# Layer 1's output projection with five chunks in space of their own, activation tables asked for ahead of use, and a reordered layer norm with filler transposes

## The chip, the core and the metric

The kernel runs on one NeuronCore of a Trainium2 chip. [...] The metric is the device time of one execution in microseconds; lower is better.

## The reference, cut to what matters

A decoder of two layers over 256 tokens of 1024 features, in fp32. Each layer is: a token mixer together with a memory cross-attention, one output projection, a residual and a layer norm, then a PEER channel mixer (a product-key expert layer), a residual and a layer norm.

```python
for i in range(2):
    z  = x @ w_in[i]                                   # streams of the mixer and the 4 attention queries
    hm = mlstm(z) if i == 0 else rglru(z)              # 768 of 1024 features
    ha = cross_attention(xq, mem, w_kv[i])             # the other 256
    x  = layer_norm(ALPHA * x + concat(hm, ha) @ w_out[i])   # "ln1"
    x  = layer_norm(ALPHA * x + peer_ffn(x))                 # "ln2"; starts with q = x @ w_q
```

Layer 1's mixer is a gated linear recurrence. Per channel, with r and i sigmoids of two block-diagonal projections of the convolved stream:

```python
log_a = -8 * r * softplus(-lam); a = exp(log_a)
u = sqrt(-expm1(2 * log_a)) * (i * xr)
h[t] = a[t] * h[t-1] + u[t];  y = h * gelu(gate)
```

## The kernel before, in words

Every large product is done on split operands: a weight `w` is cast to `wH` (a rounded fp32 form that PE runs at full rate) and `wL = w - wH`, the moving operand likewise, and `mm3` (L168 to L172) issues three matmuls, HH, LH and HL. All weights come by one list of items in the order of use. `load` (L119) issues their DMAs on SP into a ring of five raw buffers, `pump` (L78) casts (ACT, or DVE with `cast_dve`) and subtracts (DVE, POOL for the first `pool_cols` columns), and `next` (L137) hands one split item to the products and keeps the splitting three items ahead. Split items live in a ring of three, except those with a destination of their own: the third to fifth chunk of each `w_out` go to `self.extra` (`EXTRA = 3`). There is no scheduler: every queue's order is the order of the Python calls. Small generators placed beside a projection (`beside`, `tick`) get one step per weight item, after its splitting.

**The output projection** is `proj_n` (L188). It runs over the eight 128-row chunks of `w_out` in the order given by `ORDER`. With `tail`, the last chunks are held back: first all products of token half 0 (two banks of 512 columns) over those chunks, then those of token half 1 (banks of 512, 256 and 256 columns), and between these the layer norm's generator `norm` (L260) is stepped, so that half 0 is normalized beside half 1's products. Layer 0 holds back six chunks, layer 1 four. For half 1, the chunks in the ring come ahead of those in space of their own.

**The norm** (`early` form, L263 to L411): residual add and statistics per bank (`add`, `half`, L275 to L283), square root on ACT (L288), reciprocal (L291). Half 0's first 256 columns are scaled by ACT and POOL (`scale_beside`, L308 to L312), the next 256 by DVE (`center` L296, `spread` L301) and transposed (`turn`, L322, copies L225 and L226) beside half 1's products. After half 1's statistics, its first 256 columns are scaled and transposed; that is what the first query projection of the PEER layer (`proj_t`, 24 matmuls of 256 columns per weight item) waits for. Half 0's columns 512 to 1023 are scaled after that and transposed by later steps, beside the projection.

**Layer 1's mixer** (`rglru_layer`, L709): six block projections on PE (L229), sigmoids on ACT (L827), then for three pairs of channel groups b = 0, 1, 2: `decay(b)` (POOL multiplies i by the stream, L793; ACT takes exp and tanh, L794 and L795; DVE forms the argument of the square root, L796 and L797), `root(b)` (ACT, L801), `scan(b)` (DVE, L804 and L806) and `mixed(b)` (DVE gate product L810, cast and subtract into `mixH` and `mixL`). ACT holds one table of functions at a time; sigmoid, exp with tanh, and the square root each need their own load. The attention's transposes, copies (L490) and products stand between the parts of b = 0. `scan(2)` and `mixed(2)` are called inside the output projection, ahead of its fifth chunk, and so behind the splitting of the last three chunks on DVE and ACT.

Of the kernel before, what the change touches and what calls it, by code (L numbers as in the profile page):

```python
# [7 lines left out]
F32 = mybir.dt.float32  # L8
# [5 lines left out]
ALU = mybir.AluOpType  # L14
# [4 lines left out]
P = 128  # L19
# [15 lines left out]
MIX_COLS = 0  # L35
GAP, GAP2 = 56, 104
ORDER = [(6, 7, 0, 1, 2, 3, 4, 5), (0, 1, 6, 7, 2, 3, 4, 5)]
CAND = [(0, 1, 16, 0), (1, 1, 8, 16), (2, 1, 5, 24), (3, 1, 4, 29), (4, 1, 3, 33), (5, 3, 2, 36), (8, 8, 1, 42)]
# [7 lines left out]
class Trunk:  # L46
# [91 lines left out]
    def next(self, ahead=HL_BUFS):  # L138
        while callable(self.items[self.n_got][2]) or self.items[self.n_got][3] is not None:
            self.pump(self.n_got + 1)  # L140
            self.split.pop(self.n_got, None)
            self.n_got += 1
        i = self.n_got
        self.pump(i + ahead)
        self.n_got += 1
        self.tick()
        return self.split.pop(i)
# [14 lines left out]
    pool_cols = MIX_COLS  # L162
    put_off = None
    chained = False
# [19 lines left out]

    def proj_n(self, splits, stat, order=range(DT), tail=0, hook=(-1, None)):
# [12 lines left out]
        last = (DT - 1, DT - 1 - HL_BUFS if tail else DT - 1)  # L198
        for n, dt in enumerate(order):
            if n == hook[0]:  # L200
                hook[1]()
            late.append((n, dt, self.next(min(HL_BUFS + min(n, EXTRA), DT - n) if tail else HL_BUFS)))
            if n + 1 > DT - tail and n + 1 < DT:
                continue
            if tail and n + 1 == DT:
                break
            for tt in range(2):
                for k in range(len(parts[tt])):
                    products(tt, k, late)
            late = []  # L210
        if not tail:
            return banks
        ln = self.norm(banks, False, True)
        own, ring = late[:tail - HL_BUFS], late[tail - HL_BUFS:]
# [42 lines left out]
    def norm(self, y, last, early, fill=False):  # L257
# [71 lines left out]
        if last:  # L329
# [24 lines left out]
        nc.vector.tensor_scalar(nm, mv[:, 0, 0:1], rs[:, 0:1], -1.0, op0=ALU.mult, op1=ALU.mult)  # L354
# [5 lines left out]
        if fill:  # L360
            owed = []
            self.pool_cols, self.put_off = 512, owed.append
            self.pump(self.n_got + 3)
            self.put_off = None
        else:
# [29 lines left out]
        root(1)  # L395
        spread(1, 0, 1)
        turn(1, 0, 1)
        scale(1, 1, 1)
        scale(0, 2, 2), scale(1, 2, 2)
        self.release("g", "b")  # L400

        def rest():
            yield
            turn(1, 1, 1)
            yield
            turn(0, 2, 2)
            yield
            turn(1, 2, 2)
        self.beside(rest())

# [101 lines left out]
    def mlstm_layer(self):  # L512
        nc, tc, A = self.nc, self.tc, self.A
        with ExitStack() as ctx:
# [185 lines left out]
            def turn():  # L700
                for k in range(3):
# [6 lines left out]
                    self.split_to(self.flat2(self.mixH, k), self.flat2(self.mixL, k), p)  # L708
            self.proj_n((512, 512), (self.mixH, self.mixL), ORDER[0], HL_BUFS + EXTRA, (2, turn))  # L709


    def rglru_layer(self):
        nc, tc, A = self.nc, self.tc, self.A
        with ExitStack() as ctx:
# [49 lines left out]
            def values():  # L764
                for c in (2, 3):
# [12 lines left out]
            self.extra = [(w2.tile([P, D], F32R, name=f"eH{i}"), w2.tile([P, D], F32R, name=f"eL{i}"))  # L778
                          for i in range(EXTRA)]
            rr = w2.tile([P, 2, 6, T], F32, name="rr")  # L780
            aa = w2.tile([P, 6, T], F32, name="aa")
            th = w2.tile([P, 6, T], F32, name="th")
            for b in range(3):
                nc.scalar.activation(gt[:, 2 * b:2 * b + 2, :].rearrange("p a b -> p (a b)"), gb[b], AF.Gelu)
            dve = nc.vector.tensor_copy
            self.cast_dve = True
            self.pump(self.n_got + 2 + EXTRA)
            self.cast_dve = False
            fl = lambda t, b: t[:, 2 * b:2 * b + 2, :].rearrange("p a b -> p (a b)")

            def decay(b):
                for i in (2 * b, 2 * b + 1):
                    nc.gpsimd.tensor_mul(rr[:, 1, i, :], xc[:, i, :], rr[:, 1, i, :])  # L793
                    nc.scalar.activation(aa[:, i, :], rr[:, 0, i, :], AF.Exp, scale=c8[:, i:i + 1])  # L794
                    nc.scalar.activation(th[:, i, :], rr[:, 0, i, :], AF.Tanh, scale=n8[:, i:i + 1])  # L795
                nc.vector.tensor_mul(fl(rr[:, 0], b), fl(aa, b), fl(aa, b))  # L796
                nc.vector.scalar_tensor_tensor(fl(th, b), fl(rr[:, 0], b), 1.0, fl(th, b),  # L797
# [393 lines left out]
    def plan(self):  # L1191
# [24 lines left out]
        def tail(layer):  # L1216
            for i, dt in enumerate(ORDER[layer]):
                self.add(A["w_out"][layer, dt], D, i - 2 if 0 <= i - 2 < EXTRA else None)
            norm("ln1", layer)
# [119 lines left out]
```

## Time and profile before

| | us |
|---|---|
| median of three runs (1837.09 to 1838.29) | 1837.71 |
| the profiled execution, its own time | 1837.36 |
| span of its trace | 1835.5 |
| PE busy in the span | 1805.2 |
| DVE, ACT, POOL busy | 1301.6, 942.6, 430.2 |

The span runs from the first instruction to the last; the profiled execution's own time lies 1.9 us above it, and 0.35 us under the median. Times in rows of the timeline are microseconds from the span's start: start, length, engine, line, operation, output and inputs; a bracket gives the idle time of that engine just before and whose instruction ended it. Rows of PE in the timeline are pipelined, so that two of them overlap and the distance of their starts is what one costs. In rows of the windows, the columns are the stretch, its length, busy time (and count) of PE, the granted PE clock (1.00 is full), the share of DMA time and GB/s. A row of the waits is: who waited for whom, total us, times, longest us.

### The profile page before, as it was taken

The page shows a single profiled execution, that of the slowest core. Times are in us where ns is not written, and L with a number is a line of the kernel's source. Part 1 is how long each engine was busy: PE and PEld are TensorE (multiplying, and loading weights), DVE is VectorE, ACT ScalarE, POOL GpSimd, SP SyncE. Part 2 cuts the span into 40 slices and gives each one's busy share as a digit, 9 for nine tenths or more (in the row PEclk, how much of TensorE's full clock was granted, in tenths as well). Part 3 has the DMA queues.
Part 4 walks back from the last instruction along what each step waited for, and adds up shares of the span by engine and source line. Part 5 has one row for each costly group of instructions (what it writes and reads, how often), then busy time and mean ns, then how long its engine had stood idle before and what let it go on. Part 6 is the DMA issues. An engine that isn't in the chain of part 4 may idle for free.

```text
span 1835.5 us, 33243 instructions
## 1 busy us (share of the span) xinstructions
PE 1805.2 (98%) x12756; PEld 1666.0 (91%) x12756; DVE 1301.6 (71%) x2659; ACT 942.6 (51%) x1613; POOL 430.2 (23%) x324
## 2 busy tenths in 40 slices
PE   8999999999999999999999899999999999999998
PEld 8999999999999888888898799999999988888886
DVE  6673679599998555666678648785999965555556
ACT  6554555455544555555557355554555454555443
POOL 2015762433331000100001368335333300000000
PEclk9999999999999999999999899999999999999999
DMA  7655566655555666667644355666555566666664
GB/s 238 205 159 187 173 195 189 195 171 162 162 162 170 195 192 193 193 218 228 206 167 150 119 174 182 195 195 186 161 162 161 162 183 195 194 192 193 192 195 136
DMA packets 95551, 334.19 MB, mean 182 GB/s; under 512 B 10652, under 2 KB 13728, under 8 KB 95136
## 3 DMA queue, kind: packets, MB, share of 16 engines
q1 hardware_dynamic: 93752, 328.93, 58.7%
q10 hardware_dynamic: 1640, 3.15, 0.5%
q8 instruction: 99, 1.62, 0.4%
q14 instruction: 60, 0.49, 0.1%
HBM read 330.98 MB, written 1.05 MB: 181 GB/s over the span
## 4 chain that ended last, share of the span: by engine, by line
PE 72%; issue 17%; POOL 7%; DVE 2%; ACT 1%; DMA 1%; SPq 0%; POOLq 0%; DVEq 0%; ACTq 0%
PE bank L172 23%; PE bank L170 23%; PE bank L171 23%; POOL wL L108 7%; PE bank L229 2%; DMA raw<-in_w0kg_dram 0%; ACT wH L98 0%; PE bank L322 0%; POOL wL L111 0%; DVE wL L113 0%; DVE x L275 0%; SPq L127 0%; DVE x L296 0%; DMA cp<-in_rg_par_dram 0%; DVE x L301 0%
## 5 line engine op out<-in xcount | busy, mean ns | idle before, releaser
L98 ACT CAST wH<-raw 128x1024 fp32r<-128x1024 f32 (+2 forms) x607 | 628.6, 1037 | 772.3 <-PE bank L172 321.0
L113 DVE TENSOR_TENSOR wL<-raw,wH 128x1024 fp32r<-128x1024 f32 (+3 forms) x413 | 464.8, 1128 | 446.4 <-ACT wH L98 433.6
L170 PE MATMUL bank<-xHL,wH 128*128 128x256 f32 x2536 | 717.3, 283 | 7.1 <-ACT wH L98 6.2
L172 PE MATMUL bank<-xHL,wL 128*128 128x256 f32 x2536 | 703.9, 278 | 0.6 <-DVE wL L113 0.5
L171 PE MATMUL bank<-xHL,wH 128*128 128x256 f32 x2536 | 704.2, 278 | 0.0
L170 PEld LDWEIGHTS bank<-xHL,wH 128*128 128x128 f32 x2536 | 478.9, 189 | 7.9 <-ACT wH L98 6.2
L172 PEld LDWEIGHTS bank<-xHL,wL 128*128 128x128 f32 x2536 | 478.7, 189 | 1.4 <-DVE wL L113 1.0
L171 PEld LDWEIGHTS bank<-xHL,wH 128*128 128x128 f32 x2536 | 479.4, 189 | 0.4 <-DVE xHL L226 0.3
L171 PE MATMUL bank<-wL,cH 128*128 128x512 f32 x1015 | 394.3, 388 | 0.0
L170 PE MATMUL bank<-wH,cH 128*128 128x512 f32 x1015 | 394.3, 388 | 0.0
L172 PE MATMUL bank<-wH,cL 128*128 128x512 f32 x1015 | 394.3, 388 | 0.0
L111 POOL TENSOR_TENSOR wL<-raw,wH 128x1024 fp32r<-128x1024 f32 (+1 forms) x121 | 257.3, 2129 | 212.3 <-ACT wH L98 211.4
L171 PEld LDWEIGHTS bank<-wL,cH 128*128 128x128 f32 x1015 | 190.5, 188 | 39.6
L170 PEld LDWEIGHTS bank<-wH,cH 128*128 128x128 f32 x1015 | 190.5, 188 | 39.2
L172 PEld LDWEIGHTS bank<-wH,cL 128*128 128x128 f32 x1015 | 190.5, 188 | 39.1
L108 POOL TENSOR_TENSOR wL<-raw,wH 128x386 fp32r<-128x386 f32 x126 | 129.5, 1027 | 280.1 <-DVE wL L106 280.1
L311 POOL TENSOR_TENSOR x<-x,raw 128x256 f32<-128x256 f32 x6 | 4.8, 803 | 559.9 <-ACT x L308 559.9
L966 DVE TENSOR_TENSOR oh<-iota,i12T 128x1024 f16<-128x1024 f16 x128 | 130.4, 1018 | 0.0
L106 DVE TENSOR_TENSOR wL<-raw,wH 128x640 fp32r<-128x640 f32 x126 | 104.0, 825 | 7.6
L969 DVE TENSOR_TENSOR oh<-oh,gT 128x1024 f16<-128x1024 f16 x128 | 90.0, 703 | 4.4
L1099 PE MATMUL bank<-oh 128*128 128x128 f16 x1024 | 80.9, 220 | 1.1 <-DVE oh L969 1.1
L1099 PEld LDWEIGHTS <-oh 128*128 128x128 f16 x1024 | 58.8, 97 | 6.0 <-DVE oh L969 1.5
(276 smaller groups left out, 1534.3 us busy)
## 6 DMA issues: line engine op xcount, KB each, us to landing
raw<-in_u_dram SPq DMA_DIRECT2D x256, 512.0 KB, 3.6
raw<-in_v_dram SPq DMA_DIRECT2D x256, 512.0 KB, 4.3
raw<-in_w_q_dram SPq DMA_DIRECT2D x32, 512.0 KB, 3.9
raw<-in_w_out_dram SPq DMA_DIRECT2D x16, 512.0 KB, 4.1
raw<-in_w0qx_dram SPq DMA_DIRECT2D x8, 512.0 KB, 5.0
raw<-in_wkv_dram SPq DMA_DIRECT2D x8, 512.0 KB, 4.6
raw<-in_w0v_dram SPq DMA_DIRECT2D x8, 384.0 KB, 6.2
raw<-in_w0o_dram SPq DMA_DIRECT2D x8, 384.0 KB, 3.1
```

The source lines that it names most:

```text
L98: (nc.vector.tensor_copy if self.cast_dve else nc.scalar.copy)(h[:, c], r[:, c])
L106: nc.vector.tensor_sub(l[:, k:], r[:, k:], h[:, k:].bitcast(F32))
L108: nc.gpsimd.tensor_sub(l[:, :k], r[:, :k], h[:, :k].bitcast(F32))
L111: nc.gpsimd.tensor_sub(l[:, :k], r[:, :k], h[:, :k].bitcast(F32))
L113: rest = lambda l=l, r=r, h=h, k=k: nc.vector.tensor_sub(l[:, k:], r[:, k:], h[:, k:].bitcast(F32))
L170: mm(out, sH, mH, start=start, stop=False, skip_group_check=True)
L171: mm(out, sH, mL, start=False, stop=False, skip_group_check=True)
L172: mm(out, sL, mH, start=False, stop=stop, skip_group_check=True)
L229: self.nc.tensor.matmul(out, lhsT, rhs, start=start, stop=stop, skip_group_check=True)
L966: nc.vector.tensor_tensor(flat(oh[:, 1:3]), self.iota2.unsqueeze(1).to_broadcast([P, 4, P, 2]), pairs(self.i12T[:, j]), op=ALU.is_equal)
L969: nc.vector.tensor_tensor(flat(oh[:, 0:2]), two.rearrange("p z (q e t) -> p z q e t", q=2, t=2), pairs(self.gT[:, j]), op=ALU.mult)
L1099: nc.tensor.matmul(wp[:, qs], oh[:, 2, q // 2, :, q % 2], oh[:, z, q // 2, :, q % 2], start=z == 0, stop=z == 1, skip_group_check=True)
```

## The change

Five edits.

1. `EXTRAS = (3, 5)`: layer 1's `w_out` has five chunks in space of their own instead of three, its first seven chunks are split before the products start (two more by DVE, ahead of `decay(0)`), and layer 1 holds back five chunks instead of four. In half 1 one ring chunk is followed by four own chunks (before: three and one).
2. Layer 1's mixer is reordered. One-element activations ask for the sigmoid table right after the gelus and for the square root's table right after the exponentials; `decay` is cut into ACT's and POOL's part and DVE's part `grown`; `scan(0)` stands ahead of the attention's copies; `scan(2)` and `mixed(2)` come before the output projection instead of inside it; the casts of `mixed(1)` and `mixed(2)` move from ACT to DVE.
3. The early norm, both layers: all of half 0 is scaled (DVE columns 256 to 1023) and transposed beside half 1's products. Half 1's first two 128-column pieces are scaled, transposed and copied one by one, with 22 filler transposes of the identity on PE ahead of them and 5 behind. One of the two weight splits issued there gives POOL 512 instead of 1024 columns, with DVE's part called later.
4. The remaining transposes are stepped by `ahead`, before the splitting of the next item instead of after it.
5. At the start, the first two pieces of `x` transposed are loaded into raw buffers instead of into `qT`'s space.

```diff
+FILL = (22, 5)
+EXTRAS = (EXTRA, 5)
@@ next
         i = self.n_got
+        if self.ahead:
+            next(self.ahead, None)
         self.pump(i + ahead)
@@ proj_n
-        last = (DT - 1, DT - 1 - HL_BUFS if tail else DT - 1)
+        n_ring = DT - 2 - extra
+        last = (DT - 1, DT - 1 - n_ring if tail else DT - 1)
-        own, ring = late[:tail - HL_BUFS], late[tail - HL_BUFS:]
+        own, ring = late[:-n_ring], late[-n_ring:]
+    def idle(self, n):
+        b = self.bank()
+        for _ in range(n):
+            self.nc.tensor.transpose(b[:, :P], self.ident, self.ident)
@@ norm
-        if early:
-            root(0)
-            scale(0, 1, 1)
-        else:
+        if fill:
             yield
             part = add(1, 0)
-            root(0)
+        root(0)
         nc.vector.tensor_scalar(nm, mv[:, 0, 0:1], rs[:, 0:1], -1.0, op0=ALU.mult, op1=ALU.mult)
         scale_beside(0, 1 if early else 2)
         if early:
+            scale(0, 1, 1), scale(0, 2, 2)
             yield
             part = add(1, 0)
         half(*part)
-            self.pool_cols = D
-            self.pump(self.n_got + 4)
+        owed = []
+        if early:
+            self.pool_cols = D
+            self.pump(self.n_got + 3)
+        self.pool_cols, self.put_off = 512, owed.append
+        self.pump(self.n_got + 3 + early)
+        self.put_off = None
         if early:
-            turn(0, 0, 2)
+            turn(0, 0, 2), turn(0, 2, 2)
...
         center(1, 0, 1)
         root(1)
-        spread(1, 0, 1)
-        turn(1, 0, 1)
+        ps = [self.bank() for _ in range(2)]
+        for dt in range(2):
+            ds = slice(dt * P, (dt + 1) * P)
+            nc.vector.scalar_tensor_tensor(x[:, 1, ds], x[:, 1, ds], rs[:, 1:2], b[:, ds], op0=ALU.mult, op1=ALU.add)
+        self.idle(FILL[0])
+        for dt in range(2):
+            nc.tensor.transpose(ps[dt][:, :P], x[:, 1, dt * P:(dt + 1) * P], self.ident)
+            nc.scalar.copy(self.xH[:, dt, P:], ps[dt][:, :P])
+        for dt in range(2):
+            nc.vector.tensor_sub(self.xL[:, dt, P:], ps[dt][:, :P], self.xH[:, dt, P:].bitcast(F32))
+        self.idle(FILL[1])
+        owed.pop()()
         scale(1, 1, 1)
-        scale(0, 2, 2), scale(1, 2, 2)
+        scale(1, 2, 2)
@@ rglru_layer
+            nc.scalar.activation(junk, self.eps, AF.Sigmoid)
-            self.cast_dve = True
-            self.pump(self.n_got + 2 + EXTRA)
-            self.cast_dve = False
+
+            def early(n):
+                self.cast_dve = True
+                self.pump(self.n_got + n)
+                self.cast_dve = False
+            early(5)
@@ 
-            decay(0)
-            root(0)
+            early(7)
+            decay(0), nc.scalar.activation(junk, self.eps, AF.Sqrt)
+            grown(0), root(0), scan(0)
             self.xattn_turn(w2, dve)
             for co in range(3, 6):
                 gate(co, rest[co - 3])
-            scan(0)
             first, last = self.xattn_out(0), self.xattn_out(1)
             mixed(0, dve)
             self.split_to(*first, dve)
+            decay(1), decay(2), nc.scalar.activation(junk, self.eps, AF.Sqrt)
+            for b in (1, 2):
+                grown(b), root(b)
             self.split_to(*last, dve)
-            for b in (1, 2):
-                decay(b)
-            for b in (1, 2):
-                root(b)
-            scan(1)
-            mixed(1)
-            self.proj_n((512, 512), (self.mixH, self.mixL), ORDER[1], HL_BUFS + 1,
-                        (4, lambda: (scan(2), mixed(2))))
+            scan(1), mixed(1, dve)
+            scan(2), mixed(2, dve)
+            self.proj_n((512, 512), (self.mixH, self.mixL), ORDER[1], 5, EXTRAS[1])
@@ plan
-            to.stage = lambda dt=dt: self.qT[:, dt, :]
+            if dt > 1:
+                to.stage = lambda dt=dt: self.qT[:, dt, :]
```

More of the change, by code (lines that the diff above doesn't have):

```diff
@@ L162 @@
     pool_cols = MIX_COLS
-    put_off = None
+    put_off = ahead = None
     chained = False
@@ L183, in proj_t, with proj_n @@
         return banks
-    def proj_n(self, splits, stat, order=range(DT), tail=0, hook=(-1, None)):
+    def proj_n(self, splits, stat, order=range(DT), tail=0, extra=EXTRA, hook=(-1, None)):
         sH, sL = stat
@@ L201, in proj_n @@
                 hook[1]()
-            late.append((n, dt, self.next(min(HL_BUFS + min(n, EXTRA), DT - n) if tail else HL_BUFS)))
+            late.append((n, dt, self.next(min(HL_BUFS + min(n, extra), DT - n) if tail else HL_BUFS)))
             if n + 1 > DT - tail and n + 1 < DT:
@@ L359, in norm @@
         half(*part)
-        if fill:
-            owed = []
-            self.pool_cols, self.put_off = 512, owed.append
+        owed = []
+        if early:
+            self.pool_cols = D
             self.pump(self.n_got + 3)
-            self.put_off = None
-        else:
-            self.pool_cols = D
-            self.pump(self.n_got + 4)
+        self.pool_cols, self.put_off = 512, owed.append
+        self.pump(self.n_got + 3 + early)
+        self.put_off = None
         self.pool_cols = MIX_COLS
         if early:
-            turn(0, 0, 2)
+            turn(0, 0, 2), turn(0, 2, 2)
         yield
@@ L405, in rest @@
             yield
-            turn(0, 2, 2)
             yield
             turn(1, 2, 2)
-        self.beside(rest())
+            yield
+            self.ahead = None
+        self.ahead = rest()
     def mem_k(self, kb, c, h, l):
@@ L708, in turn @@
                     self.split_to(self.flat2(self.mixH, k), self.flat2(self.mixL, k), p)
-            self.proj_n((512, 512), (self.mixH, self.mixL), ORDER[0], HL_BUFS + EXTRA, (2, turn))
+            self.proj_n((512, 512), (self.mixH, self.mixL), ORDER[0], HL_BUFS + EXTRA, EXTRA, (2, turn))
     def rglru_layer(self):
@@ L778, in rglru_layer @@
             self.extra = [(w2.tile([P, D], F32R, name=f"eH{i}"), w2.tile([P, D], F32R, name=f"eL{i}"))
-                          for i in range(EXTRA)]
+                          for i in range(EXTRAS[1])]
             rr = w2.tile([P, 2, 6, T], F32, name="rr")
@@ L795, in decay, with grown @@
                     nc.scalar.activation(th[:, i, :], rr[:, 0, i, :], AF.Tanh, scale=n8[:, i:i + 1])
+            def grown(b):
                 nc.vector.tensor_mul(fl(rr[:, 0], b), fl(aa, b), fl(aa, b))
@@ L1217, in tail @@
             for i, dt in enumerate(ORDER[layer]):
-                self.add(A["w_out"][layer, dt], D, i - 2 if 0 <= i - 2 < EXTRA else None)
+                self.add(A["w_out"][layer, dt], D, i - 2 if 0 <= i - 2 < EXTRAS[layer] else None)
             norm("ln1", layer)
```

## The prediction

> **What bounds the kernel now.** I read the page first, then PE's waits, then the timeline around each of them, then the granted clock in windows. The page (PE's row of its first part, and a DMA row):
>
> ```profile
> PE 1805.2 (98%) x12756; PEld 1666.0 (91%) x12756; DVE 1301.6 (71%) x2659; ACT 942.6 (51%) x1613; POOL 430.2 (23%) x324
> ...
> raw<-in_w_out_dram SPq DMA_DIRECT2D x16, 512.0 KB, 4.1
> ```
>
> PE is idle for 2% of the span, some 30 us, so an edit away from PE's gaps is worth nothing. PE's waits over the whole span name nearly all of those gaps:
>
> ```profile
> PE bank L322 <- DVE x L301: 7.3, 3, 4.1
> PE bank L170 <- ACT wH L98: 6.2, 1, 6.2
> PE bank L170 <- ACT mixH L225: 3.3, 1, 3.3
> PE bank L170 <- DVE mixH L225: 2.2, 1, 2.2
> ```
>
> L322 is a transpose of the early norm (one wait in layer 0, two in layer 1), 6.2 is the kernel's start, and both `mixH` rows are layer 1's mixer. The change edits exactly these places. Idle time has a second price, shown by the granted clock (fourth column; the third is PE's busy time):
>
> ```profile
> 136.03:139.44 3.41, 1.46 (x13) 1.00 0.49 151
> ...
> 142.85:146.27 3.42, 3.42 (x18) 0.50 0.02 6
> ...
> 1002.99:1006.40 3.41, 1.99 (x8) 1.00 0.00 0
> ...
> 1016.65:1020.06 3.41, 1.39 (x7) 1.00 0.88 276
> ...
> 1023.47:1026.89 3.42, 3.42 (x9) 0.50 0.02 5
> ...
> 1040.55:1043.96 3.41, 3.41 (x17) 0.50 0.20 67
> ```
>
> The clock halves at the end of a 3.41 us stretch in which PE was busy 1.39 or 1.46 us, and not after one with 1.99 us; it comes back at the end of a fully busy stretch. So three times (layer 0's norm, layer 1's mixer, layer 1's norm) some 4 to 6 us of matmuls run at 0.50.
>
> [...]
>
> **Layer 1's mixer.** Timeline rows, times in us:
>
> ```profile
> 978.86 8.45 SPq L127 DMA_DIRECT2D raw<-in_w_out_dram  x5
> ...
> 986.87 0.69 DVE L98 CAST eH<-raw 128x1024 fp32r<-128x1024 f32 x1
> ...
> 988.74 0.69 DVE L98 CAST eH<-raw 128x1024 fp32r<-128x1024 f32 x1
> ...
> 994.86 0.69 DVE L796 TENSOR_TENSOR rr<-aa 128x512 f32<-128x512 f32 x1 [3.78 <-ACT th L795]
> ...
> 996.36 1.28 ACT L801 ACT_TABLE_LOAD   x1 [1.53 <-DVE th L797]
> ...
> 997.65 0.72 ACT L801 ACTIVATE th<-th,tiny 128x512 f32<-128x512 f32 x1
> ...
> 997.45 2.48 DVE L490 COPY pT<-bank 128x512 f32<-128x512 f32 x4 [1.18 <-PE bank L487]
> ...
> 1003.43 0.83 DVE L225 CAST mixH<-gt 128x512 fp32r<-128x512 f32 x1
> ...
> 1004.41 0.47 PE L170 MATMUL bank<-wH,mixH 128*128 128x512 f32 x1 [2.23 <-DVE mixH L225]
> ...
> 1007.47 0.40 PE L170 MATMUL bank<-wH,mixH 128*128 128x512 f32 x1
> ...
> 1010.25 0.40 PE L170 MATMUL bank<-eH,mixH 128*128 128x512 f32 x1
> ...
> 1014.46 3.50 DVE L113 TENSOR_TENSOR wL<-raw,wH 128x1024 fp32r<-128x1024 f32 x3 [0.26 <-ACT wH L98]
> ...
> 1018.59 1.27 DVE L806 TENSOR_TENSOR_SCAN aa<-aa,th 128x256 f32<-128x256 f32 x2
> ...
> 1021.29 0.79 PE L170 MATMUL bank<-wH,mixH 128*128 128x512 f32 x1 [3.25 <-ACT mixH L225]
> ```
>
> *Two more chunks split early.* One cast with its subtraction costs DVE 1.87 (start to start of the casts), two 3.74. They fall into the 3.78 that DVE idles before 994.86: cost 0. Without that cover everything behind on DVE would slip. SP issued the last `w_out` loads by 987.3, and one lands in 4.1, so the data are there.
>
> *Table loads.* The square root of b = 0 waited 1.28 for its table (996.36 to 997.64) after DVE had finished. Asked for right after the tanh, the load runs beside `grown(0)`: 1.3 saved on that path, and again before `root(1)`. The early sigmoid saves nothing, for the block products behind it set the time. POOL's multiplies move only with ACT. [...]
>
> *DVE's chain, rewritten,* with 0.69 for every 512-column operation: `grown(0)` ends at 996.25, its root at 997.0, `scan(0)` (0.69 + 1.27) at 998.95, the four copies at 1001.45, `mixed(0)`'s product and cast at 1002.95. PE starts there instead of at 1004.41. Then: its subtraction 0.69, first attention split 0.76 (half of 0.83 + 0.69), `grown(1)` and `grown(2)` 2.76, second split 0.76, `scan(1)` 1.96, `mixed(1)` 2.21, `scan(2)` 1.96, product and cast of `mixed(2)` 1.52: 1015.55. The 0.83 was taken while POOL ran; the 1024-column cast takes 0.69, so 512 columns may cost 0.35. I take the middle for the last two: `mixed(2)` at 1015.1, bounds 1014.6 to 1016. Before, it came at 1021.29, held by the three splits (3.50) and the ACT cast, which are gone from its path.
>
> *PE.* A chunk costs 2.78 (1007.47 to 1010.25), each half of its columns for each token half 0.69. Three chunks from 1002.95, 0.2 for `mixL`, and three shares of 0.69 end at 1013.6; then a new wait of 1.5 for `mixed(2)` in place of 3.25. Behind it stand 0.69, four shares of bank 1 (2.78) and the ring chunk (1.39), plus 0.2 for `mixL`: half 0 ends at 1020.2.
>
> **The norms.** Timeline, layer 1, the last three rows layer 0:
>
> ```profile
> 996.82 1.91 PE L487 MATMUL bank<-ident,pr 128*128 128x128 f32 x16
> ...
> 1027.63 0.69 DVE L275 SCALAR_TENSOR_TENSOR x<-x,bank 128x512 f32<-128x512 f32 x1 [1.96 <-PE bank L172]
> ...
> 1030.90 0.60 ACT L308 ACTIVATE x<-x,nm,rs 128x256 f32<-128x256 f32 x1 [1.29 <-DVE nm L354]
> ...
> 1032.39 0.73 POOL L312 TENSOR_TENSOR x<-x,raw 128x256 f32<-128x256 f32 x1
> ...
> 1034.49 0.69 DVE L226 TENSOR_TENSOR xHL<-bank,xHL 128x512 fp32r<-128x512 f32 x1 [0.50 <-ACT xHL L225]
> ...
> 1038.69 0.69 PE L322 MATMUL bank<-ident,x 128*128 128x128 f32 x2 [4.14 <-DVE x L301]
> ...
> 1039.84 0.58 PE L170 MATMUL bank<-xHL,wH 128*128 128x256 f32 x1 [0.46 <-ACT xHL L225]
> ...
> 1041.07 1.77 DVE L296 SCALAR_TENSOR_TENSOR x<-x,mv,raw 128x512 f32<-128x512 f32 x1
> ...
> 1042.88 0.75 DVE L301 SCALAR_TENSOR_TENSOR x<-x,rs,raw 128x512 f32<-128x512 f32 x1
> ...
> 137.72 0.40 DVE L275 SCALAR_TENSOR_TENSOR x<-x,bank 128x256 f32<-128x256 f32 x1
> ...
> 140.15 0.66 PE L322 MATMUL bank<-ident,x 128*128 128x128 f32 x2 [2.65 <-DVE x L301]
> ...
> 141.27 0.58 PE L170 MATMUL bank<-xHL,wH 128*128 128x256 f32 x1 [0.46 <-ACT xHL L225]
> ```
>
> *Layer 1.* The add of bank 1 waits for bank 0's add and statistics: 1020.9 instead of 1027.63, 6.7 earlier. ACT's scale came 3.27 after it; two 256-column operations (about 0.95) move behind it, so 1023.25, and POOL's products, 2.2 later, at 1025.5. DVE then does that pair (1024.2) and the new 512-column pair: 0.75 + 0.75 quiet, 1.77 + 0.75 as beside POOL; I take 1026.4. PE reaches the transposes at 1020.2 + 1.39 + 2.78 = 1024.4, so a second new wait of 1.6 to 2 (before: 0.7). A transpose costs 0.11 (1.91 for 16, less the last one's tail), eight 0.9; 24 matmuls follow and end at 1029.6. DVE: add and statistics 1.4, two subtractions 1.38, the next quarter 0.8: the last quarter's add at 1030.0. From that add to the first query matmul layer 0 took 3.55 (137.72 to 141.27); with 128-column pieces and transposes at full clock I take 3.2: restart at 1033.2 against 1039.84, **6.6 saved**.
>
> *Fillers.* 22 of 0.11 are 2.4: 1029.6 to 1032.0, while the first piece comes at about 1032.2, so they delay nothing; the five behind run beside the copy and the subtraction. If DVE were sooner, each would cost 0.11. They keep PE busy through the gap, so the clock should stay: the stretch at 0.50 ran from 1039.84 to 1043.96, half of it is **2.05 saved**. The moved transposes of half 0 leave the busy stream for waiting time, **0.4 saved**.
>
> *Layer 0.* No mixer gain, and one subtraction of 0.69 more ahead of the last add: restart at 138.4 + 3.2 = 141.6, **0.3 lost**; the clock (141.27 to 146.27 at half) **2.5**, the transposes **0.4 saved**. Its six held chunks cover the new 512-column pair.
>
> *Splits.* POOL's load drops by half a split and DVE takes it later, 0.69; with the clock full, PE also reaches the third weight item 2 us sooner, and DVE's queue is then just in time: **0.3 lost**. `ahead` puts the transposes' copies before the casts on ACT, which costs nothing there, as PE is 2.8 behind.
>
> **The start.** Timeline:
>
> ```profile
> 1.29 0.29 DVE L249 CAST iota<-fi 128x256 f16<-128x256 int32 x1
> ...
> 1.61 0.39 SPq L127 DMA_DIRECT2D qT<-in_xT_dram  x1
> ```
>
> `qT` lies on space that the constants' setup used, and the first DMA goes out right after DVE's last use of it (1.58). A raw buffer has no such past. Bounds: 1.6 if SP is free from the span's start, nothing if something else holds it as long. I take the middle, **0.8**, as all of PE's first wait (6.2) hangs on that DMA. The fourth and fifth weight loads now wait for the first two splits, and land later by at most half a microsecond, 1 us before PE needs them.
>
> **Sum.** 6.6 + 2.05 + 0.4 (layer 1), 2.6 (layer 0), 0.8, less 0.3: 12.1. The profiled execution took 1837.36, 0.35 under the median: 1825.3, on the median's footing 1825.5.
>
> **Rivals.**
> *A: the two new waits of layer 1 cost the clock.* 1.5 and 1.6 us in a 3.41 stretch leave 1.8 to 1.9 busy, between the 1.46 that lost it and the 1.99 that kept it. One loss is 1.7 to 2.5, both 4: 1829.5.
> *B: the fillers don't hold the clock.* They read one constant tile, and no row shows transposes alone. Then they run at half rate, some 2.9 longer in each layer, and 2.5 and 2.05 are not saved: 10.4 dearer, 1836. [...]
> *C: the mixer gains less.* If DVE's chain meets POOL throughout, `mixed(2)` comes 3 to 4 later: 1829.
> *D: slower.* DVE's queue stands behind the two early casts: if their loads came late by S, decay, scans, products, norm all slip by S. It decides from S = 12 for no gain, 16 for 0.2% slower: 1842. Against it: 4.1 to landing, and five raw buffers whose turn comes by 987.
>
> **How the numbers follow.** Forecast 0.70 (alone 1821.5 to 1829), A 0.12, B 0.06, C 0.05, D 0.07. The bound of what can be told from no change is 0.2%, 3.7 us. Faster: forecast, A, C and half of B, 0.90; same: half of B, 0.03; slower: D, 0.07. The range 1821 to 1833 holds forecast, A and C with the unknown cast, contention and start; B, D and the tails are left out.
>
> **What would show it.** Right: DVE busy without a gap from 991 to 995; no table load between DVE's `grown` and the root; `mixH`'s last cast about 6 us earlier, on DVE; PE's waits 1 to 2 us in the mixer and at the norm's transposes; granted clock 1.00 through both norms; PE's first matmul near 5.4. Wrong: windows at 0.50 behind the fillers (B) or inside layer 1's held products (A), a wait for DMA before the two casts (D), the last cast of `mixH` less than 3 us earlier (C).

## The result and the profile after

The changed kernel took 1825.52 us (median of four, 1825.24 to 1825.91), against 1837.92 (1837.09 to 1838.29) for the kernel before beside it: a ratio of 0.9933, with a 95% interval of 0.9916 to 0.995. The prediction was 1825.5 in a range of 1821 to 1833. The sum was right; several of its steps were not, and their errors cancelled, so that it agrees to 0.02 is luck. The spans are 1823.7 against 1835.5, so the traces have 11.8 us to tell of.

In the rows PE is the matrix engine, DVE the vector engine, ACT the one for activation functions and copies, POOL a second engine for elementwise work, and SP issues the DMAs. PE's waits over the whole span of the changed kernel (who waited for whom: us in total, times, longest):

```profile
PE bank L174 <- ACT wH L100: 4.8, 1, 4.8
PE bank L240 <- DVE pT L509: 2.1, 1, 2.1
PE bank L333 <- POOL x L323: 1.7, 1, 1.7
...
PE bank L174 <- DVE mixH L236: 0.6, 1, 0.6
...
PE bank L333 <- DVE x L312: 0.5, 1, 0.5
PE bank L410 <- DVE x L407: 0.2, 1, 0.2
```

The four waits the prediction started from (7.3, 6.2, 3.3, 2.2) have become 2.4 at the norms' transposes (1.7, 0.5 and 0.2), 4.8 at the start and 0.6 in the mixer. The 0.5 is the third wait of the 7.3; the prediction counted it to layer 1's early norm, but it belongs to the norm between the layers (at 932.15 before, 928.55 after), which the change leaves as it is. And there is a new wait of 2.1 that the prediction does not have: PE waits for `pT`, the copies of the attention's transposes.

To see where the 11.8 us lie, I cut both spans at three rows of PE, each named by the start of its work: the first query product after layer 0's norm (141.27 before, 140.32 after), the first of the 56 gate products of layer 1 (984.73, 981.15), and the first query product after layer 1's norm (1039.84, 1030.32).

| stretch | before | after | saved | forecast |
|---|---|---|---|---|
| start to layer 0's restart | 141.27 | 140.32 | 0.95 | 0.8 - 0.3 = 0.5 |
| to layer 1's gate products | 843.46 | 840.83 | 2.63 | 2.5 + 0.4 = 2.9 |
| layer 1's mixer and norm, to the restart | 55.11 | 49.17 | 5.94 | 6.6 |
| the rest | 795.66 | 793.38 | 2.28 | 2.05 + 0.4 - 0.3 = 2.15 |

Each figure is of one execution. In four other traces with the same code up to layer 0's restart (`three_own`, `four_own`, `turn_first`, `no_asks` below) it stands at 140.51 to 140.91 instead of 140.32, so the first row is good to some 0.6 us.

The clock. Windows of PE after (stretch, length, busy time and count, granted clock, DMA share, GB/s): layer 0's fillers and what follows, then in layer 1 a stretch laid by hand around the longest wait of its norm, the fillers, and what follows:

```profile
136.71:140.13 3.42, 3.24 (x29) 1.00 0.42 140
140.13:143.54 3.41, 3.34 (x30) 1.00 0.46 118
...
1020.20:1023.60 3.40, 1.74 (x10) 1.00 0.00 0
1027.01:1030.42 3.41, 3.41 (x32) 1.00 0.41 144
1030.42:1033.83 3.41, 3.32 (x30) 1.00 0.54 151
```

The clock is 1.00 behind both sets of fillers (rival B would have shown 0.50), and the 1.66 us wait of the norm, which leaves 1.74 busy, did not cost it either (rival A). Nor did the 2.14 us wait for `pT`, though a stretch laid around it (995.00 to 998.41) has PE busy only 1.27, less than the 1.39 and 1.46 that lost the clock before: such a stretch alone doesn't decide.

The mixer after, timeline (start, length, engine, line, operation, output and input; in brackets the idle time before and who ended it):

```profile
986.58 2.77 POOL L816 TENSOR_TENSOR rr<-xc,rr 128x256 f32<-128x256 f32 x2 [0.76 <-ACT rr L852]
...
987.54 1.22 DVE L100 CAST eH<-raw 128x1024 fp32r<-128x1024 f32 x1
988.80 1.64 DVE L115 TENSOR_TENSOR eL<-raw,eH 128x1024 fp32r<-128x1024 f32 x1
990.36 0.68 DVE L100 CAST eH<-raw 128x1024 fp32r<-128x1024 f32 x1
991.07 1.23 DVE L115 TENSOR_TENSOR eL<-raw,eH 128x1024 fp32r<-128x1024 f32 x1
992.21 0.68 DVE L821 TENSOR_TENSOR rr<-aa 128x512 f32<-128x512 f32 x1
...
990.75 0.49 ACT L818 ACTIVATE th<-rr,n 128x256 f32<-128x256 f32 x1
991.26 1.28 ACT L858 ACT_TABLE_LOAD   x1
...
993.72 0.73 ACT L826 ACTIVATE th<-th,tiny 128x512 f32<-128x512 f32 x1 [0.96 <-DVE th L822]
...
996.46 2.46 DVE L509 COPY pT<-bank 128x512 f32<-128x512 f32 x4
...
997.27 3.69 PE L240 MATMUL bank<-pT,vm 128*128 128x256 f32 x16 [2.14 <-DVE pT L509]
1000.62 0.59 PE L174 MATMUL bank<-wH,mixH 128*128 128x512 f32 x1
...
1011.49 0.43 DVE L236 CAST mixH<-gt 128x512 fp32r<-128x512 f32 x1
...
1011.97 0.50 PE L174 MATMUL bank<-eH,mixH 128*128 128x512 f32 x1 [0.58 <-DVE mixH L236]
...
1017.98 0.67 DVE L286 SCALAR_TENSOR_TENSOR x<-x,bank 128x512 f32<-128x512 f32 x1
```

The table load runs between the exponentials and `grown(0)`, as foreseen. But DVE reaches `grown(0)` (992.21) 0.97 after the tanh before it (990.75 + 0.49), held by the two extra splits; beside POOL a cast took 1.22 and a subtraction 1.64, where 0.68 and 1.23 stand in the next two rows. PE then does not go from the copies into the output projection: the attention's 16 products stand between, and wait 2.14 for the copies. (Their operands are plain fp32, and their 256 columns cost 0.21 each, 997.27 to 1000.62 for 16. Products of the rounded form, also of 256 columns, start 0.11 apart in the stretch behind 1030.66, about as many columns per us as the f16 products: eight of 128 columns in 0.44 at 373.29 of the kernel before.)

The norm of layer 1 after:

```profile
1023.09 1.20 PE L333 MATMUL bank<-ident,x 128*128 128x128 f32 x8 [1.66 <-POOL x L323]
...
1027.01 2.56 PE L233 MATMUL bank<-ident 128*128 128x128 f32 x22
...
1027.21 0.42 DVE L286 SCALAR_TENSOR_TENSOR x<-x,bank 128x256 f32<-128x256 f32 x1 [0.26 <-PE bank L176]
...
1030.32 0.36 PE L174 MATMUL bank<-xHL,wH 128*128 128x256 f32 x1
```

### The profile page after: what moved, and what is told of

Read it like the earlier page. It is cut to its first block, busy times and chain, and to the rows that moved or that the text cites. A ratio compares the mean times of both kernels' runs of the same rounds, so it can differ in the third digit from the quotient of the medians.

```text
span 1823.7 us, 33361 instructions
## 1 busy us (share of the span) xinstructions
PE 1804.1 (99%) x12810; PEld 1666.1 (91%) x12810; DVE 1307.6 (72%) x2669; ACT 940.7 (52%) x1614; POOL 429.2 (24%) x324
## 3 DMA queue, kind: packets, MB, share of 16 engines
q8 instruction: 100, 1.64, 0.4%
## 4 chain that ended last, share of the span: by engine, by line
PE 73%; issue 17%; POOL 7%; DVE 2%; ACT 1%; DMA 0%; POOLq 0%; SPq 0%; DVEq 0%; ACTq 0%
PE bank L176 23%; PE bank L174 23%; PE bank L175 23%; POOL wL L110 7%; PE bank L240 2%; ACT wH L100 0%; DVE eL L115 0%; PE bank L333 0%; DVE eH L100 0%; POOL wL L113 0%; PE bank L233 0%; DMA cp<-in_rg_par_dram 0%; DMA raw<-in_w0kg_dram 0%; DVE x L286 0%; DVE wL L115 0%
```

## The experiments

The theory was the prediction's: the mixer is worth some 5 us of restart, the fillers hold the clock, the table requests and the start are worth about one each. Each experiment is judged by its time, and by the stretch it edits: the mixer and norm of layer 1, from the gate products to the restart (55.11 before, 49.17 after). The kernels ran in four groups, each beside the kernel before, whose medians there lie between 1837.73 and 1838.16; a difference between kernels of different groups is good to some 0.4 us.

### Each part alone

Three kernels hold one part of the change each. `start_alone` is the kernel before with

```diff
-            to.stage = lambda dt=dt: self.qT[:, dt, :]
+            if dt > 1:
+                to.stage = lambda dt=dt: self.qT[:, dt, :]
```

> The kernel before with only the start edit (the first two pieces of x transposed go to raw buffers). Theory: the changed kernel's layer 0 stood 1.1 us earlier at its first layer norm (127.59 against 128.68), and all of it comes from this edit: 1836.7 to 1836.9, with PE's first matmul near 4.8 and the activation table loaded before the first data. Rival: only the DMA's 0.9 us comes from the edit, or the clock's phase ate or gave some of it: 1837.2 or more. No effect: 1837.9.

`norm_alone` has the norm's rewrite, `ahead` and the fillers, with three own chunks and the old mixer:

```diff
+        self.idle(FILL[0])
         for dt in range(2):
             nc.tensor.transpose(ps[dt][:, :P], x[:, 1, dt * P:(dt + 1) * P], self.ident)
...
-            self.proj_n((512, 512), (self.mixH, self.mixL), ORDER[1], HL_BUFS + 1,
+            self.proj_n((512, 512), (self.mixH, self.mixL), ORDER[1], HL_BUFS + 1, EXTRA,
```

> The kernel before with only the norm edits (half 0 scaled early, 128-column pieces, fillers, ahead, the split put off); mixer, three own chunks and start as before. Theory: layer 0 gains its 2.5 us, layer 1's first query matmul comes no sooner (half 0 still ends at about 1027.5 and DVE's chain is as long), and the clock gives 2.3 there if the fillers cover the gap: 1833.1; PE's work ends some 1.9 us before the first piece is ready, so the clock may be lost there: then 1835.4. Rival (the norm edits make the restart sooner by themselves, as much as in the changed kernel): 1829.

`mixer_alone` has the five own chunks and the new order of the mixer, with the old norm:

```diff
+            early(7)
+            decay(0), nc.scalar.activation(junk, self.eps, AF.Sqrt)
+            grown(0), root(0), scan(0)
...
+            self.proj_n((512, 512), (self.mixH, self.mixL), ORDER[1], 5, EXTRAS[1])
```

> The kernel before with only layer 1's mixer and output projection edits (five own chunks, tables asked for, the new order); norms and start as before. Theory: half 0 ends 6 us earlier, the query projection starts 5.7 us earlier and loses the clock as before: 1832.2. The three parts alone then give 1.1 + 4.8 + 5.7 = 11.6 of 12.4 measured together. Rival (the parts need each other: a longer held tail without the early scaling makes PE wait for POOL, and most of the gain goes): 1835.

Measured, beside the kernel before at 1837.98 (median of 22):

| | us (range) | ratio, 95% | saved |
|---|---|---|---|
| start_alone | 1836.78 (1834.5 to 1838.25) | 0.9992, 0.9983 to 1.0001 | 1.2 |
| norm_alone | 1831.79 (1830.12 to 1833.36) | 0.9968, 0.9956 to 0.998 | 6.2 |
| mixer_alone | 1833.33 (1830.77 to 1835.75) | 0.998, 0.9971 to 0.9989 | 4.65 |

The sum of the three, 12.05, is close to what they give together (12.4). The intervals are some 2 us to either side for each part, and that of `start_alone` holds no change at all, so this shows no large interaction, and no more. PE's waits of `mixer_alone`:

```profile
PE bank L331 <- DVE x L310: 5.5, 3, 2.7
PE bank L238 <- DVE pT L499: 2.1, 1, 2.1
```

The old wait of the norms is back (5.5), and the wait for `pT` comes with the mixer's new order; the mixer's stretch is 49.69. The norm gives half of the whole gain, but little of it as an earlier restart: with `norm_alone` the mixer's stretch is 53.71, 1.4 shorter (where I had expected nothing), while layer 0's stretch (840.72) and the rest (793.89) are 2.74 and 1.77 shorter, as the clock is kept there (the start to layer 0's restart was 0.91 longer in that execution).

### The fillers

```diff
-        self.idle(FILL[0])
...
-        self.idle(FILL[1])
```

> The changed kernel without its 27 filler transposes in each norm. Theory: PE then idles some 2.4 to 2.7 us before the pieces, the clock halves (a 3.41 us stretch with PE busy under 1.46 us lost it before) and each layer loses about 2.3: 1830 if both do, 1827.5 to 1828 if one does, by where the gap falls in the window. [...]

Without them: 1828.43 (1828.16 to 1830.6; ratio to the kernel before 0.9954, 0.9941 to 0.9968), 2.9 slower than with them. Its windows, at layer 0's and layer 1's norm:

```profile
137.50:140.90 3.40, 0.76 (x3) 1.00 0.29 104
140.90:144.30 3.40, 3.40 (x16) 0.50 0.56 170
1028.40:1031.80 3.40, 1.15 (x9) 1.00 0.47 154
1031.80:1035.20 3.40, 3.35 (x15) 0.50 0.30 87
```

PE's waits for the first piece, from the timeline:

```profile
139.98 0.50 PE L409 MATMUL bank<-ident,x 128*128 128x128 f32 x2 [2.67 <-DVE x L407]
...
1031.38 0.63 PE L409 MATMUL bank<-ident,x 128*128 128x128 f32 x2 [2.25 <-DVE x L407]
```

The clock halves (1.00 to 0.50) behind both gaps, of 2.67 and 2.25, so the fillers do hold it. The slow stretches last 3.4 here, 6.8 in the kernel before, and what follows the two norms is 1.63 and 1.26 longer than with fillers (842.46 and 794.64), where the prediction had 2.5 and 2.05 from the kernel before.

Twice as many:

```diff
-FILL = (22, 5)
+FILL = (44, 5)
```

> The changed kernel with 44 fillers instead of 22 ahead of the two pieces. Theory: 22 just cover the gap (0.2 us of waiting left in layer 0, none in layer 1), so 22 more cost 22 x 0.11 = 2.4 us in each layer, less 0.2: 1830.1. Rival (a filler costs half of that, or there is room for more): 1827.5 or less.

1830.39 (1829.69 to 1832.05; 0.996, 0.9947 to 0.9974), 4.9 slower, with the mixer and norm at 51.36 instead of 49.17: 2.19 more. That is 22 of 0.11 less 0.2, as both pieces are then ready and PE transposes them in 0.38 instead of 0.59. So 22 just fill the gap, and each one more costs 0.1 in each layer.

### The table requests

```diff
-            nc.scalar.activation(junk, self.eps, AF.Sigmoid)
...
-            decay(0), nc.scalar.activation(junk, self.eps, AF.Sqrt)
+            decay(0)
...
-            decay(1), decay(2), nc.scalar.activation(junk, self.eps, AF.Sqrt)
+            decay(1), decay(2)
```

> The changed kernel without the three early table requests. Theory (a load costs the 1.28 us of its row and nothing beside it): the first square root starts 1.25 us later, everything on DVE behind it slips by that, and the second load was 0.2 us from being needed anyway: 1826.7. [...] Rival (hidden anyway): 1825.5.

1828.01 (1826.88 to 1829.36; 0.9947, 0.9933 to 0.996), 2.5 slower. Its timeline, then its windows:

```profile
994.17 1.28 ACT L825 ACT_TABLE_LOAD   x1 [2.33 <-DVE th L821]
995.47 0.72 ACT L825 ACTIVATE th<-th,tiny 128x512 f32<-128x512 f32 x1
...
999.02 5.38 PE L240 MATMUL bank<-pT,vm 128*128 128x256 f32 x16 [3.28 <-DVE pT L509]
...
1013.36 0.43 DVE L236 CAST mixH<-gt 128x512 fp32r<-128x512 f32 x1
```

```profile
997.20:1000.60 3.40, 1.58 (x6) 1.41 (x7) 3.40 (x7) 3.37 (x8) 2.17 (x3) 0.90 0.00 0
1000.60:1004.00 3.40, 3.40 (x11) 2.73 (x10) 3.26 (x8) 3.39 (x9) 0.00 (x1) 0.60 0.00 0
```

(In these windows PE, PEld (PE's weight loads), DVE, ACT and POOL stand in this order before the clock.) The table load stands again between DVE's `grown` and the root, 1.28 on DVE's chain: from the gate products (981.75 here, 981.15 after) to the last cast of `mixH` it is 31.61 instead of 30.34. On top, PE's wait for `pT` grows to 3.28 and costs the clock (0.90 and 0.60). The stretch is 50.84, 1.67 longer. In the time alone, 1828.01, the requests are worth more than the 1.2 I expected (1826.7), but the rows show no cost of the load itself beyond its 1.28: the root starts 0.02 after its load's end, and the chain is 1.27 longer. The rest of the spans' difference (1825.9 against 1823.7) lies ahead of layer 0's restart (140.91 against 140.32), where the code is the same.

### The two splits that were costed at nothing

With three own chunks and four held, the two early splits are gone:

```diff
-EXTRAS = (EXTRA, 5)
+EXTRAS = (EXTRA, 3)
...
-            early(7)
...
-            self.proj_n((512, 512), (self.mixH, self.mixL), ORDER[1], 5, EXTRAS[1])
+            self.proj_n((512, 512), (self.mixH, self.mixL), ORDER[1], 4, EXTRAS[1])
```

> The changed kernel with three own chunks and four held ones in layer 1, as before; everything else as changed. Theory: DVE has two chunks less ahead of decay (0.9 us sooner, for the two cost 4.67 us against 3.78 of idle time), but three splits of 1.2 us each come behind the last mixed product; half 0 ends 0.9 later, with its first bank sooner for it, the chain through DVE is the same: 1825.3 if the clock holds, 1827 if PE's some 2 us of idling behind the fillers lose it. So the space alone is worth nothing or the clock. Rival (the space is what brings the mixer's gain, 3.5 us of splits): 1829.

1825.36 (1825.17 to 1825.85; 0.9932, 0.9918 to 0.9946): no difference from five. DVE's timeline:

```profile
991.53 0.69 DVE L821 TENSOR_TENSOR rr<-aa 128x512 f32<-128x512 f32 x1 [3.65 <-ACT th L818]
...
1011.90 3.49 DVE L115 TENSOR_TENSOR wL<-raw,wH 128x1024 fp32r<-128x1024 f32 x3
```

`grown(0)` now starts when ACT is done, with 3.65 idle before it. That shows that the two splits are what kept it late, and the last cast of `mixH` comes 0.90 sooner after the gate products (29.44 against 30.34). But three subtractions (3.49) then stand behind `mixed(2)` instead of one, and most of the 0.9 is lost there: the stretch is 48.89.

Between the two lies four:

```diff
-EXTRAS = (EXTRA, 5)
+EXTRAS = (EXTRA, 4)
...
-            early(7)
+            early(6)
```

> The changed kernel with four chunks of their own instead of five in layer 1's mixer, and two split in the ring. With five, the last early subtraction ended 0.93 us after the tanh that grown(0) waits for; with three, DVE was free in time but two more subtractions stood behind mixed(2), and the time came out the same (1825.36). Four leave one early split less (1.9 us, enough for the 0.93) and one more late one (1.2 us, beside 2.87 us in which DVE idled). If DVE's chain sets the mixer's time: grown(0) starts right after the tanh, the output projection about 0.7 earlier, the last add about 0.9 earlier, time 1824.6. If the mixer's time is set elsewhere (by PE's products from the first mixH on, or by the products of the norm): 1825.4 as with three and five.

1823.23 (1822.75 to 1824.32; 0.9919, 0.9906 to 0.9933), 2.3 faster than the changed kernel (its slowest run is faster than that kernel's fastest, 1825.24), more than the 0.9 I expected. PE's waits and its timeline:

```profile
PE bank L240 <- DVE pT L509: 1.2, 1, 1.2
```

```profile
1021.63 1.21 PE L333 MATMUL bank<-ident,x 128*128 128x128 f32 x8 [0.32 <-POOL x L323]
...
1028.50 0.36 PE L174 MATMUL bank<-xHL,wH 128*128 128x256 f32 x1
```

From the gate products (981.42) to the restart it is 47.08, 2.09 shorter. The wait for `pT` fell by 0.94, as the theory has it. What I had not seen is that the number of own chunks also sets the order of PE's work. The chunks that `mixed(2)` makes (4 and 5 of `ORDER`) now both come by the ring, so own chunks 7, 2 and 3 fill the time until it is there, and the wait of 0.58 for the last `mixH` is gone; the same two ring chunks put 0.7 more of PE's work ahead of the norm's transposes, and the wait for POOL falls from 1.66 to 0.32. DVE's chain alone does not give it: the last cast of `mixH` comes 29.41 behind the gate products, as in `three_own` (29.44), whose stretch is 1.81 longer with one more subtraction (1.14) behind that cast and another order of the chunks. No run parts these two.

### The copies ahead of the scan

```diff
-            grown(0), root(0), scan(0)
+            grown(0), root(0)
             self.xattn_turn(w2, dve)
+            scan(0)
```

> The changed kernel with the attention's transposes and copies ahead of the first scan again. Theory: DVE idled 0.92 us waiting for the first root, and the copies fill that; PE does its attention products 2 us sooner and then waits for the first mixed product; DVE's chain ends 0.7 us sooner: 1824.9. Rival (the order of the first scan is what the mixer's gain rests on): 1826.5 or more.

1826.42 (1825.68 to 1827.31; 0.9938, 0.9924 to 0.9951): not faster, and the stretch is 49.82, 0.65 longer. The wait for `pT` is gone, but (timeline):

```profile
997.46 3.00 POOL L816 TENSOR_TENSOR rr<-xc,rr 128x256 f32<-128x256 f32 x3 [7.32 <-ACT rr L852]
...
997.78 2.16 DVE L831 TENSOR_TENSOR_SCAN aa<-aa,th 128x256 f32<-128x256 f32 x2
...
1001.62 0.47 PE L174 MATMUL bank<-wH,mixH 128*128 128x512 f32 x1 [2.23 <-DVE mixH L236]
```

The scans, 1.27 in the changed kernel, took 2.16 beside POOL's products, which in the changed kernel run beside the copies (2.46 there; 2.48 here, without POOL); and PE waits 2.23 for the first `mixH` instead of 2.14 for `pT`. From the gate products to the last cast of `mixH` it is 30.99 instead of 30.34, all of the 0.65: here DVE's chain sets the mixer, and PE's wait in it is only where that shows.

### The wait for POOL, and DVE's queue in the norm

```diff
-        for k in range(3):
-            products(1, k, own), next(ln, None)
+        products(1, 0, own), products(1, 1, own)
+        next(ln, None), next(ln, None)
+        products(1, 2, own), next(ln, None)
```

> The changed kernel with one edit in the norm of the mixers: PE does the held chunks' products of the second quarter ahead of the transposes of token half 0 instead of behind them, so 1.4 us of work fills the 1.7 us in which PE waited for POOL's products. If PE's waits are what the norm costs: 1.4 us less, 1824.1. If DVE's queue sets the last add (its adds and statistics stand behind the two subtractions of the split, 1.27 us): the last add comes 0.26 earlier, when DVE has got to it, and the time is 1825.2.

The place answers; the time fits neither value. PE's waits, then two windows:

```profile
PE bank L411 <- DVE x L408: 1.9, 2, 0.9
```

```profile
996.48:999.89 3.41, 2.51 (x8) 0.78 0.00 0
999.89:1003.30 3.41, 3.41 (x13) 0.72 0.00 0
```

The 1.66 became 0.27, and 1.7 came back as waits for the pieces (0.2 became 1.9 in the two layers together): the last add came 8.92 after the second one (1018.61 to 1027.53), 9.23 in the changed kernel, 0.31 earlier as DVE's queue allows, not 1.4. The time was 1826.82 (1825.89 to 1827.97; 0.994, 0.9926 to 0.9953), 1.3 slower: in the profiled execution the wait of 2.14 for `pT`, the same as in the changed kernel, lost the clock (0.78, 0.72), and the stretch is 49.37, 0.2 longer. That execution took 1825.89, the fastest of the five; where the rest of the 1.3 lies is open.

With four own chunks, this order, and the subtractions behind the last statistics:

```diff
...
-            turn(0, 0, 2), turn(0, 2, 2)
+            turn(0, 0, 2, lows), turn(0, 2, 2, lows)
...
+        for f in lows[:1]:
+            f()
         for dt in range(2):
...
+        for f in lows[1:]:
+            f()
         self.idle(FILL[1])
```

> Four own chunks, the order of norm_order, and DVE's two low-half subtractions of token half 0 put behind the last statistics: one in the wait for ScalarE's cast of the last piece, one behind the pieces. If DVE's queue sets the last add, the add comes 1.27 + 0.26 + 0.7 earlier than in the changed kernel, about 0.5 is given back at the next transposes, whose scaling DVE reaches later: 1823.8 +- 0.4. If it is the subtraction behind the pieces that the first query products wait for, the gain is eaten: 1824.6, as four chunks alone.

```profile
1027.37 0.36 PE L174 MATMUL bank<-xHL,wH 128*128 128x256 f32 x1
...
1030.90 0.44 PE L334 MATMUL bank<-ident,x 128*128 128x128 f32 x2 [0.47 <-DVE x L313]
```

The stretch is 46.04, 1.04 shorter than with four chunks alone, and 0.47 is waited at the next transposes. The time does not show it: 1824.04 (1822.96 to 1824.31; 0.9923, 0.991 to 0.9937), which can't be told from `four_own`, although the one profiled execution was the fastest of its five. So work taken out of DVE's queue ahead of the last add brings the restart forward, and whether that is worth having in the time stays open.

## Why the prediction was right, and where it was not

The forecast of 1825.5 stands beside 1825.52. The four stretches miss by 0.45, -0.27, -0.66 and 0.13 of saving, 0.35 too little in all; the kernel before came out at 1837.92 instead of the 1837.71 that the sum started from, and the rest is within the scatter. What carried the result was the mechanism: an earlier end of DVE's chain in the mixer, a shorter norm, and a clock that is kept.

*The start* was right in size and short of a cause. The first DMA goes out at 0.74 instead of 1.61, 0.87 earlier and within the bounds given (nothing to 1.6). But PE's first matmul comes 1.39 earlier (4.79 against 6.18): ACT's first table load, which started only at 3.96 before, with the data of `qT`, now runs at once and is done before the data are there (2.94):

```profile
0.73 1.28 ACT L100 ACT_TABLE_LOAD   x1 [0.73 <-PEq L1352]
0.74 0.39 SPq L129 DMA_DIRECT2D raw<-in_xT_dram  x1
...
4.79 0.58 PE L174 MATMUL bank<-xHL,wH 128*128 128x256 f32 x1 [4.79 <-ACT wH L100]
```

At the second add of layer 0's norm 1.09 of it is left (127.59 against 128.68). In `start_alone` the restart of layer 0 (140.99) is only 0.28 earlier, though its first matmul is 1.70 earlier. PE's matmuls of 256 columns start 0.21 apart until 9.79 there, until 9.56 in the kernel before and until 9.45 in the changed one, and 0.11 apart after that. So in these three traces the slow time of the start ends at about the same moment, whether the first matmul comes at 4.48, 6.18 or 4.79, and an earlier one does its work at the slow rate (the granted clock of the windows reads 1.00 there, so only the distances show it). What the edit is worth in time stays open: `start_alone` can't be told from no change.

*Layer 0* was right: 2.49 in all (0.14 lost at the restart, 2.63 saved by the clock and the moved transposes) against 2.6, to the 0.6 by which such stretches differ between traces.

*"Two more chunks split early: cost 0"* failed. DVE's durations were taken from rows without POOL; POOL's products of `decay(0)` fall on just these splits, and the 3.78 of cover did not do. It cost 0.9 at `grown(0)` (`three_own`).

*"PE starts there instead of at 1004.41"* failed. The step took the output projection to follow DVE's first cast. Between them stand the attention's 16 products, which wait for copies that the change put behind `scan(0)`. PE started at 1000.62, which is 1004.2 in the old count (times after plus 3.58, by which the changed kernel is ahead at the gate products): 0.2 gained, not 1.46. The new wait I did forecast in the mixer, 1.5 for `mixed(2)`, was 0.58 for the same reason: PE itself came later.

*DVE's chain* was right on balance. `mixed(2)`'s cast ended at 1011.92, 1015.5 in the old count, against 1015.1 in the forecast and 1021.29 before. The three casts took 0.43 each, where I had counted 0.83 and taken 0.45 off for two of them; the other 0.75 gave back most of the 0.9. As this chain sets the mixer (`turn_first`, `no_asks`), PE's missed 1.26 did not reach the end: the second add stood at 1021.56 in the old count, 0.66 later than forecast.

*The table loads* were right in mechanism: 1.28 on the chain, 1.67 with the clock that the longer wait then costs. In the kernel before, the rows show a load of 1.28 at each change: sigmoid at 986.78, exp and tanh at 991.83, the square root at 996.36, then the same three again at 998.39, 1002.00 and 1007.97. The second load, for which the prediction counted another 1.3, was not on the chain: of 2.6 the chain shows 1.27.

*The norm of layer 1* was right, with one slip. The second new wait was 1.66 (1.6 to 2 forecast), the last add to restart 3.11 (3.2). The last add waited for PE (0.26), not for DVE as the step said, but `norm_order` shows DVE just behind. The slip is in the sum: transposes at 1026.4, 0.9 for eight and 2.9 for 24 matmuls of 0.12 end at 1030.2, not at 1029.6, and so behind the add at 1030.0. The restart was at 1033.9 in the old count against 1033.2, 5.94 saved of 6.6.

*The fillers* were right: they hold the clock, and cost 0.2 at most (the stretch is 48.96 without them).

*The rivals.* B is refuted (clock 1.00 behind the fillers), D too (no wait for a DMA before the two splits), C did not come: DVE met POOL in the early splits and in the copies, which took no longer for it. A did not come in the profiled execution, but its mechanism exists, at another place and at a lower price: the wait of 2.14 at `pT` lost the clock in `norm_order`, for some 0.5 (the second add 37.36 behind the gate products instead of 36.83), because DVE's chain and not PE sets what follows.

## What to carry to other kernels

A cover is a time and a set of neighbours: splits that fill an engine's idle time exactly are only free if their durations come from rows with the same engine running beside them (here a cast took 0.68 alone and 1.22 beside POOL). Where a vector engine's chain sets a stage, PE's waits in it are symptoms; filling or moving one (`turn_first`, `norm_order`) gave nothing here, while a shorter chain did (`no_asks` the other way). Changing how many buffers a stage owns also changes the order of the consumer's work: three and five chunks took the same time here, four took 2.3 us less. Fillers on the matrix engine paid here when they ended just before the work they bridge to (2.9 in the time), and cost nearly their full length beyond that (22 more, 2.4 long, made layer 1's stretch 2.19 longer).

## What was not expected of the hardware

- *The same wait lost the clock in one kernel and not in another.* Behind the wait of 2.14 at `pT` the changed kernel kept it (1.00 from 996.48 to 1003.30, the 16 products took 3.69). `norm_order`, with the same 2.14, lost it: 0.78 and 0.72 over two stretches of 3.41, and 5.38 for the 16 products. `mixer_alone`, with 2.1, shows 0.91 from 1005 to 1006. What decides between them was not shown.
- *The time at half clock differs.* In the kernel before it lasts 6.83 behind layer 0's norm (139.44 to 146.27), 6.83 in the mixer (1020.06 to 1026.89) and 6.82 behind layer 1's norm (1037.14 to 1043.96), in `no_fillers` 3.4 each time (from 140.9 and from 1031.8). In `no_fillers` PE was busy for 3.40 and 3.35 of it; in the kernel before for 2.24, 2.18 and 1.40 of its first half and throughout the second. From run to run the kernel before took 1836.02 to 1840.52 over 22 runs and 1837.09 to 1838.29 over four, the changed one 1825.24 to 1825.91 over four. What this scatter comes from stays open, as does the difference of single stretches: from layer 0's restart to layer 1's gate products the changed kernel took 840.83 and `turn_first`, with the same code there, 841.44, at a mean granted clock of 0.999 over either execution.
- *Transposes of a constant hold the clock* as products do: 22 in 2.56 us, granted clock 1.00 behind them.
- *DVE beside POOL slows by kind.* A 128x1024 cast went from 0.68 to 1.22, two 256-column scans from 1.27 to 2.16, a subtraction from 1.23 to 1.64, while four copies from PE's banks (PSUM) took 2.46 beside POOL and 2.48 without. That POOL is the cause is read from which rows overlap; no run took POOL's work away.
